# Turning the S5 states back on TensorE: four products in 64-row tiles instead of two after a VectorE combination, and the norm's squares summed on TensorE, in a two-block network on one Trainium2 core

## The chip, the cores and the metric

The kernel runs on one NeuronCore of a Trainium2 chip. The metric is device microseconds of one execution. The kernel before takes 1884.67 us (median of 3 runs, 1882.24 to 1885.48). The engines are called PE (TensorE matmuls), PEld (TensorE weight loads), DVE (VectorE), ACT (ScalarE), POOL (GpSimd) and SP (SyncE, here a DMA queue).

## The reference, cut to what matters

Two blocks of two layers each run one after the other on a state of 512 tokens by 1024 channels. The change touches the end of the first block (a residual and an RMS norm with the gain of `final_norm`) and the S5 mixer that follows it:

```
bur = einsum('gnh,btgh->btgn', bb_r, uc)          # 64 groups, 16 inputs, 64 complex states each
bui = einsum('gnh,btgh->btgn', bb_i, uc)
pr, pi, sr, si = associative_scan(combine, (ar, ai, bur, bui), axis=1)   # x[t] = a * x[t-1] + bu[t], complex
y = einsum('ghn,btgn->btgh', c_re, xr) - einsum('ghn,btgn->btgh', c_im, xi)
y = gelu(y + d * u);  ab = y @ w_glu;  mix = ab[..., :dm] * sigmoid(ab[..., dm:])
```

In front of the mixer stand two norms in a row, so that two sums over the 1024 channels are needed for each token: of the squares, and of the squares times the squared gain `g_fin1`.

## The kernel before, in words

Channels lie on partitions, tokens along the free axis, in tiles of 128 by 512. Large products are made by `mm3` (lines 308 to 310): three fp32r matmuls of 128x128 weights on 512 columns (weights and inputs each split into a high and a low part). Weights come through SP's queue into two `raw` buffers (line 288), ACT makes the high part (line 249), DVE or POOL the low part (line 252), each in 3 buffers.

The stages are `even` (conv and pool mixer), `odd` (LRU mixer), `s5`, `glu`, and then MLP, gate, attention, MLP, gate and the last norm. While `even` runs, `tables` builds the S5 tables in DRAM for 8 feature tiles `ft` of 8 groups each: `tS` (inputs to states), `tM` (inputs to outputs inside a chunk), `tR` (rotations: cosine and sine for each of 64 chunks) and `tO` (states to outputs). `tO` is written by `stored` (line 1072) on SP's queue, 8 DMAs of 64 KB per `ft`, so that the real states of two groups and their imaginary states stand on 128 rows.

The last part of `odd` makes 8 output tiles `m`, 36 matmuls each. `odd_out` adds the residual on DVE, turns the tile and writes it through DRAM to make `U[m]` (the S5 input), and squares it twice on ACT, once plain and once with the gain; DVE adds each square to one of two running sums `acc12`. In `s5`, behind four filler blocks of 6 matmuls (`fillers`: the projections for the gate stages), `columns` (line 368) sums the two over the partitions with 8 matmuls of one column; then a chain of small DVE operations makes the norm factors, eight matmuls spread them (line 1197) and the tiles `U` are scaled.

`s5` then goes through `ft` = 0..7. `states(ft)` has 16 matmuls on PE (line 1251: fp32, 128 rows by 64 weight columns, on 64 columns), which leave the real parts (r = 0) and the imaginary parts (r = 1) of the chunk inputs in PSUM, the even group of a pair on rows 0 to 63 and the odd one on rows 64 to 127. DVE rotates them with `C` and `N` (three multiplications, an addition, a subtraction), scans them (line 1266), and turns them back: three multiplications into `c` and `b`, a memset, and four additions or subtractions of 64 rows each that write into another half of the rows. These build `e`: for each half `q` of the groups the real states on rows 0 to 63 and the imaginary ones on rows 64 to 127. `leave(ft)` adds, for each of the 8 groups g = 2*a4 + q, the products M*u (line 1291) and O*e (line 1293) in PSUM, two matmuls each (64 output rows `f` a time), and ACT makes the gelu. The result goes through DRAM (`dy`) and is split for the `glu` products.

The order on PE is written down by hand with `self.after()` (an instruction stands behind the last one of PE issued so far): states(0), three blocks, states(1), leave(0), a block, states(2), leave(1), a block, and so on; behind leave(5) and later the first `glu` products (`part`) stand as well. Within these bounds a scheduler sets the order. DVE's `states(ft)` is kept behind all of `states(ft - 1)`.

Of the kernel before, what the change touches and what calls it, by code (L numbers as in the profile page):

```python
# [11 lines left out]
AF = mybir.ActivationFunctionType  # L12
# [156 lines left out]
class Kern:  # L169
# [238 lines left out]
    def consts(self):  # L408
        nc = self.nc
        self.vecs = self.p_const.tile([128, self.I["vecs"].shape[1]], F32, name="vecs")  # L410
        nc.sync.dma_start(out=self.vecs, in_=self.I["vecs"])
        ct = self.p_const.tile([128, self.I["consts"].shape[1]], F32, name="ctile")
        nc.scalar.dma_start(out=ct, in_=self.I["consts"])
        C = lambda n: ct[:, self.cat[n][0]:self.cat[n][0] + self.cat[n][1]]
        self.ident, self.fix, self.eye16, self.chunk, self.not0 = (C(n) for n in ("ident", "fix", "eye16", "chunk", "not0"))
        self.half, self.own = C("half"), C("own")
        self.halfpi = self.p_const.tile([128, 1], F32, name="halfpi")
        nc.gpsimd.memset(self.halfpi, 1.5707963267948966)
        self.ones = self.p_const.tile([128, 128], F32, name="ones")
        nc.vector.memset(self.ones, 1.0)  # L420

        o = self.bank("st")
        for _ in range(self.WARM):
            nc.tensor.matmul(o[:, 0:128], self.ones, self.ones, start=True, stop=True)

        warm = self.p_const.tile([128, 1], F32, name="warm")
        self.act(warm, self.halfpi, AF.Silu)
        self.tab, self.U, self.acc12 = [], [], []
        self.ft, self.behind, self.ticks = None, [], 0


# [301 lines left out]
    def odd(self, h):  # L733
# [42 lines left out]
        for ms in self.ODD_MS:  # L776
            os = {m: self.bank(("mm", "mm", "mm", "sp", "sp", "yp", "yp", "mm")[m]) for m in ms}
            for q in range(2):
                for m in ms:
                    w = self.get_w()  # L780
                    for k in range(6):
                        self.mm3(os[m], w, k, ysp[6 * q + k], q + k == 0, q == 1 and k == 5)
                    if q == 1:
                        out[m] = self.odd_out(m, os[m], h[m])
        return out

    def lru(self, x, i, gt):
# [25 lines left out]
    def odd_out(self, m, o, h):  # L813

        n = self.H("h3")
        v = lambda a: a.rearrange("p (c s) -> p s c", s=8)
        self.add(n.rearrange("p (s c) -> p s c", s=8), v(o), v(h))
        if len(self.tab):


            r = self.L("xc", 2 + self.LAG)
            self.act(r.rearrange("p (s c) -> p s c", s=8), n.rearrange("p (s c) -> p s c", s=8)[:, ::-1], AF.Copy)
            du = self.dram.tile([128, T], F32, name=f"du{m}")
            self.nc.gpsimd.dma_start(out=du.rearrange("(s h) (g c) -> h g s c", s=8, g=8).rearrange("h g s c -> (h g) s c"),
                                     in_=r.rearrange("p (s c) -> p s c", s=8))
            U = self.p_xg.tile([128, 8, 64], F32, tag="xg", name="U")
            self.nc.gpsimd.dma_start(out=U.rearrange("p g c -> p (g c)"), in_=du)
            self.U.append(U)

            for k, g in enumerate((1.0, self.V("g_fin1", m))):  # L830
                q = self.L(*(self.sq if m else ("acc", 2)))
                self.act(q, n, AF.Square, scale=g)
                if m == 0:
                    self.acc12.append(q)
                else:
                    self.add(self.acc12[k], self.acc12[k], q)
        return n


# [19 lines left out]
    def odd_vectors(self):  # L859

        P = lambda nm, dt=F32: self.L("sv_" + nm, 1, dt, (128, 12))
        lam = self.V("lam", 0, 12)
        na, u, s, z, p, q = P("na"), P("su"), P("ss"), P("sz"), P("sp"), P("sq")
        self.act(na, lam, AF.Abs)
        self.ts(na, na, -1.0, ALU.mult)
        self.exp_small(na, 12, P, out=u)

        self.ts(q, u, 2.0, ALU.add)
        self.nc.vector.reciprocal(out=q, in_=q)
        self.mul(s, u, q)  # L870
        self.mul(z, s, s)
        self.ts(p, z, 1.0 / 15, ALU.mult)
        for c in (1 / 13, 1 / 11, 1 / 9, 1 / 7, 1 / 5, 1 / 3):
            self.stt(p, p, c, z, ALU.add, ALU.mult)
        self.stt(p, p, 1.0, s, ALU.add, ALU.mult)
        self.ts(q, lam, -1.0, ALU.mult, 0.0, ALU.max)
        self.stt(q, p, 2.0, q, ALU.mult, ALU.add)
        C = lambda nm, w: self.p_const.tile([128, w], F32, name=nm)
        self.sp4 = C("sp4", 12)
        self.ts(self.sp4, q, 4.0, ALU.mult)  # L880

# [95 lines left out]
    def tables(self, small):  # L977
# [16 lines left out]
        for ft in range(8):  # L994
# [14 lines left out]
            for q in range(2):  # L1009
# [58 lines left out]

                def stored(q=q, orr=orr, oi=oi, tO=tO):
                    for k, w in enumerate((orr, oi)):  # L1070
                        for g2 in range(2):
                            nc.sync.dma_start(out=tO[64 * k:64 * k + 64, 512 * q:512 * q + 512].rearrange("n (a g m) -> n g a m", a=2, g=2)[:, g2],
                                              in_=w[64 * g2:64 * g2 + 64].rearrange("p a j h -> p a (j h)"))

                late(stored)
                if q == 1:
# [77 lines left out]
    def s5(self, h, fill, glu):  # L1154
# [46 lines left out]
                behind(*next(blocks))  # L1201

        fillers(self.FILL[0])
        st = self.bank("st")
        for k in range(2):
            behind(self.columns, self.acc12[k], st, 4 * k)
        fillers(self.FILL[1])
        s = self.p_s.tile([128, 24], F32, tag="st", name="st_s")
        v, t = s[:, 0:8], s[:, 8:12]
# [30 lines left out]
        def states(ft):  # L1240
# [17 lines left out]
            else:  # L1258
                self.tt(a, sp, c2, ALU.mult)
            self.mul(b[:, 0], sp[:, 1], N)  # L1260
            self.mul(b[:, 1], sp[:, 0], N)
            self.add(a[:, 0], a[:, 0], b[:, 0])
            self.sub(a[:, 1], a[:, 1], b[:, 1])
            for r in range(2):
                z = a[:, r].rearrange("p a c -> p (a c)")
                nc.vector.tensor_tensor_scan(out=z, data0=dec.rearrange("p a c -> p (a c)"), data1=z, initial=0.0, op0=ALU.mult, op1=ALU.add)


            e, c = f4(), f4()
            self.tt(c, a, c2, ALU.mult)  # L1270
            self.mul(b[:, 0], a[:, 1], N, nc.gpsimd if ft in self.B0P else None)
            self.mul(b[:, 1], a[:, 0], N, nc.gpsimd if ft in self.B1P else None)
            nc.vector.memset(e[:, :, :, 0:1], 0.0)
            for r, op in ((1, ALU.add), (0, ALU.subtract)):
                for q in range(2):
                    rows = slice(64 * q, 64 * q + 64)
                    self.tt(e[64 * r:64 * r + 64, q, :, 1:64], c[rows, r, :, 0:63], b[rows, r, :, 0:63], op)
            live[ft] = O, M, u, e

        def leave(ft):  # L1280
            O, M, u, e = live.pop(ft)
# [2 lines left out]
            for q in range(2):  # L1284
                self.yps.append(self.bank("yp"))
                yp = self.yps[-1][:, 0:256].rearrange("p (a c) -> p a c", a=4)
                for a4 in range(4):
                    g = 2 * a4 + q
                    os = [yp[64 * f:64 * f + 64, a4, :] for f in range(2)]
                    for f, o in enumerate(os):  # L1290
                        nc.tensor.matmul(o, M[:, 128 * g + 64 * f:128 * g + 64 * f + 64], u[:, g, :], start=True, stop=False)
                    for f, o in enumerate(os):
                        nc.tensor.matmul(o, O[g // 4][:, g % 4, 64 * f:64 * f + 64], e[:, q, a4, :], start=False, stop=True)
                self.act(y.rearrange("p (a q) c -> p a q c", q=2)[:, :, q, :], yp, AF.Gelu_apprx_tanh)
            dy = self.dram.tile([128, T], F32, name=f"dy{ft}")
            nc.scalar.dma_start(out=dy, in_=y.rearrange("p g c -> p (g c)"))
# [533 lines left out]
```

## Time and profile before

| | |
|---|---|
| median of 3 runs | 1884.67 us (1882.24 to 1885.48) |
| the profiled execution | 1886.16 us, its span 1884.3 us |
| PE busy | 1764.2 us (94%), 9298 matmul records |
| DVE busy | 1167.2 us (62%) |
| ACT, POOL busy | 762.0 us (40%), 456.6 us (24%) |
| mean granted TensorE clock | 0.963 of 2.4 GHz |
| shares of the chain that ended last | PE 68%, DVE 14%, issue 5%, POOL 4%, ACT 4%, DMA 3% |

A row of the timeline gives the start and the duration of an instruction, its engine and source line, the tiles that it writes and reads, its shape and how many records the row merges; in brackets stands how long the engine had been idle and what released it. An fp32 matmul leaves two records, an fp32r matmul one: the 16 matmuls of `states` are a row of x32. A matmul's shape is written as rows of weights * columns of weights, then the rows and columns that it reads. `PEclk` in the table of stretches is the granted clock: 1.00 is 2.4 GHz, 0.50 is 1.2 GHz.

### The profile page before, as it was taken

What the parts mean: (1) busy time and instruction counts of PE and PEld (TensorE: products, weight loads), DVE (VectorE), ACT (ScalarE), POOL (GpSimd) and SP (SyncE); (2) the same over time, 40 slices, a digit from 0 to 9 for tenths busy, and PEclk for the clock granted to TensorE, in tenths of its full rate; (3) what the DMA queues carried; (4) which work ended last, traced back from release to release, by engine and by line L of the source; (5) the groups of instructions that cost most, each with busy time, mean ns of one, the idle gap of its engine ahead of it and who ended that gap; (6) DMA issues with size and microseconds to landing.
All of it is one profiled execution on the core that took longest, in us unless ns stands there. A gap on an engine that the chain in (4) does not pass through costs nothing.

```text
span 1884.3 us, 24650 instructions
## 1 busy us (share of the span) xinstructions
PE 1764.2 (94%) x9298; PEld 1439.7 (76%) x9298; DVE 1167.2 (62%) x1885; ACT 762.0 (40%) x1330; POOL 456.6 (24%) x422
## 2 busy tenths in 40 slices
PE   7797999999887897899999999998999999999997
PEld 5685778877765776687888888887778888888886
DVE  9989777555888859655432344578686642244456
ACT  4334444443554462234432332335665432233234
POOL 5464667333666643100000000032000000000002
PEclk8898999999988898899999999999999999999998
DMA  4598443331222488523232222333111233322322
GB/s 167 136 225 213 128 129 123 119 104 65 76 75 76 136 244 291 169 92 112 93 100 91 100 100 91 101 106 110 41 55 45 101 101 91 100 101 91 100 94 91
DMA packets 128871, 215.93 MB, mean 115 GB/s; under 512 B 40048, under 2 KB 79728, under 8 KB 128752
## 3 DMA queue, kind: packets, MB, share of 16 engines
q1 hardware_dynamic: 108144, 189.27, 32.5%
q10 hardware_dynamic: 17968, 16.43, 2.6%
q0 software_dynamic: 2640, 8.65, 1.4%
q8 instruction: 73, 1.20, 0.3%
q14 instruction: 46, 0.38, 0.1%
HBM read 187.44 MB, written 26.21 MB: 113 GB/s over the span
## 4 chain that ended last, share of the span: by engine, by line
PE 68%; DVE 14%; issue 5%; POOL 4%; ACT 4%; DMA 3%; SPq 1%; ACTq 0%; DVEq 0%; POOLq 0%
PE mm L308 19%; PE mm L310 19%; PE mm L309 19%; POOL lo L252 2%; DVE lo L252 1%; DVE e L808 1%; ACT hi L249 1%; PE pv L1609 1%; SPq L1175 1%; PE sc L309 1%; PE sc L308 1%; PE sc L310 1%; DVE pl L264 1%; DVE srm L267 1%; DVE h L264 1%
## 5 line engine op out<-in xcount | busy, mean ns | idle before, releaser
L249 ACT ACTIVATE hi<-raw 128x1024 fp32r<-128x1024 f32 (+1 forms) x280 | 292.4, 1046 | 672.8 <-PE mm L309 552.4
L252 DVE TENSOR_TENSOR lo<-raw,hi 128x1024 fp32r<-128x1024 f32 (+1 forms) x211 | 262.1, 1243 | 422.1 <-ACT hi L249 417.3
L310 PE MATMUL mm<-xg,lo 128*128 128x512 f32 x924 | 361.0, 391 | 9.4 <-DVE lo L252 8.1
L308 PE MATMUL mm<-xg,hi 128*128 128x512 f32 x924 | 363.2, 394 | 5.1 <-ACT hi L249 1.8
L309 PE MATMUL mm<-xg,hi 128*128 128x512 f32 x924 | 360.2, 390 | 0.3 <-DVE xg L252 0.2
L1423 POOL DMA_DIRECT2D pj<-proj x16 | 8.8, 549 | 1025.8 <-DVE t L264 784.0
L308 PE MATMUL mm<-hid,hi 128*128 128x512 f32 (+1 forms) x648 | 250.7, 387 | 1.8 <-DVE t L252 1.8
L309 PE MATMUL mm<-hid,hi 128*128 128x512 f32 (+1 forms) x648 | 250.3, 387 | 0.0
L310 PE MATMUL mm<-hid,lo 128*128 128x512 f32 (+1 forms) x648 | 250.1, 386 | 0.0
L310 PEld LDWEIGHTS mm<-xg,lo 128*128 128x128 f32 x924 | 173.8, 188 | 48.0 <-DVE lo L252 9.0
L308 PEld LDWEIGHTS mm<-xg,hi 128*128 128x128 f32 x924 | 173.8, 188 | 44.9 <-ACT hi L249 2.3
L252 POOL TENSOR_TENSOR lo<-raw,hi 128x1024 fp32r<-128x1024 f32 (+1 forms) x69 | 170.6, 2473 | 146.8 <-ACT hi L249 140.6
L309 PEld LDWEIGHTS mm<-xg,hi 128*128 128x128 f32 x924 | 173.8, 188 | 36.4 <-DVE xg L252 1.4
L308 PEld LDWEIGHTS mm<-hid,hi 128*128 128x128 f32 x648 | 121.7, 188 | 26.6 <-DVE t L252 2.0
L310 PEld LDWEIGHTS mm<-hid,lo 128*128 128x128 f32 x648 | 121.7, 188 | 24.6
L309 PEld LDWEIGHTS mm<-hid,hi 128*128 128x128 f32 x648 | 121.7, 188 | 24.6
L308 PE MATMUL mm<-y,hi 128*128 128x512 f32 x192 | 78.6, 409 | 10.2 <-ACT y L249 8.9
L309 PE MATMUL mm<-y,hi 128*128 128x512 f32 x192 | 76.8, 400 | 0.0
L310 PE MATMUL mm<-y,lo 128*128 128x512 f32 x192 | 76.5, 399 | 0.0
L309 PE MATMUL mm<-big,hi 128*128 128x512 f32 x160 | 64.5, 403 | 3.9 <-DVE big L264 3.9
L308 PE MATMUL mm<-big,hi 128*128 128x512 f32 x160 | 65.3, 411 | 2.2 <-ACT hi L249 2.2
L310 PE MATMUL mm<-big,lo 128*128 128x512 f32 x160 | 64.2, 402 | 0.1
(468 smaller groups left out, 3086.1 us busy)
## 6 DMA issues: line engine op xcount, KB each, us to landing
raw<-in_w_up SPq DMA_DIRECT2D x64, 512.0 KB
raw<-in_w_down SPq DMA_DIRECT2D x64, 512.0 KB
raw<-in_w_in_even SPq DMA_DIRECT2D x40, 512.0 KB
raw<-in_w_in_odd SPq DMA_DIRECT2D x24, 512.0 KB
raw<-in_w_out_even SPq DMA_DIRECT2D x16, 512.0 KB
raw<-in_w_glu SPq DMA_DIRECT2D x16, 512.0 KB
raw<-in_w_gate SPq DMA_DIRECT2D x16, 512.0 KB
raw<-in_w_out_odd SPq DMA_DIRECT2D x16, 384.0 KB
```

Source lines behind the costliest of these rows:

```text
L249: self.nc.scalar.activation(out=out, in_=in_, func=func, scale=scale, bias=bias)
L252: (eng or self.nc.vector).tensor_tensor(out=out, in0=a, in1=b, op=op)
L264: self.nc.vector.scalar_tensor_tensor(out=out, in0=a, scalar=s, in1=b, op0=op0, op1=op1)
L267: (eng or self.nc.vector).tensor_scalar(out=out, in0=a, scalar1=s1, scalar2=s2, op0=op0, **({} if op1 is None else {"op1": op1}))
L308: mm(out, hi[:, sl], xh, start=start, stop=False)
L309: mm(out, hi[:, sl], xl, start=False, stop=False)
L310: mm(out, lo[:, sl], xh, start=False, stop=stop)
L808: nc.vector.tensor_tensor_scan(out=y, data0=u[:, k], data1=x[:, k], initial=0.0, op0=ALU.mult, op1=ALU.add)
L1175: nc.sync.dma_start(out=M0[:, 128 * g:128 * g + 128], in_=bass.AP(k0.tensor, k0.offset + 4096 * g, [[16, 8], [256, 16], [1, 128]]))
L1423: self.nc.gpsimd.dma_start(out=p, in_=pj[m])
L1609: mm(o, l, r[:, w], start=n == 0, stop=n == 6 * nk - 1)
```

## The change

`states` keeps the turned states on their rows. The two tiles `c` (states times cosine) and `e` (states times plus or minus sine) are no longer combined on DVE: the memset and the four 64-row operations go, and the sign is put in by a scalar_tensor_tensor where a multiplication stood. The same is done at the first rotation, so that an addition and a subtraction of 256 columns become one addition of 512. `leave` adds up on PE what DVE combined: for each group and each output half `f`, the real rows of `c` and `e` with one half of `O`, the imaginary rows with the other, four matmuls with 64 rows of weights on 63 columns where there was one with 128 rows on 64. `tO` is written in the order in which its rows now stand, half as many DMAs. `odd_out` squares a tile once; four matmuls of two columns (ones, and the squared gain) sum it over the partitions in PSUM, over all 8 tiles.

```diff
@@ odd: behind the products of tile m
                         out[m] = self.odd_out(m, os[m], h[m])
+
+                        if m and self.squares:
+                            self.squares.pop(0)()
@@ odd_out
-            for k, g in enumerate((1.0, self.V("g_fin1", m))):
-                q = self.L(*(self.sq if m else ("acc", 2)))
-                self.act(q, n, AF.Square, scale=g)
-                if m == 0:
-                    self.acc12.append(q)
-                else:
-                    self.add(self.acc12[k], self.acc12[k], q)
+            q = self.L(*self.sq)
+            self.act(q, n, AF.Square)
+            if m == 0:
+                self.st12 = self.bank("st")
+            st = self.st12[:, 0:8].rearrange("p (j b) -> p b j", j=2)
+
+            def summed():
+                for b in range(4):
+                    with self.after():
+                        self.nc.tensor.matmul(st[:, b], q[:, 128 * b:128 * b + 128], self.g12[:, m], start=m + b == 0, stop=m == 7 and b == 3)
+
+            self.squares.append(summed)
@@ odd_vectors
+        self.g12 = C("g12", 16).rearrange("p (k j) -> p k j", j=2)
+        nc = self.nc
+        nc.vector.memset(self.g12[:, :, 0:1], 1.0)
+        self.mul(self.g12[:, :, 1], self.V("g_fin1", 0, 8), self.V("g_fin1", 0, 8))
@@ tables: stored
                     for k, w in enumerate((orr, oi)):
-                        for g2 in range(2):
-                            nc.sync.dma_start(out=tO[64 * k:64 * k + 64, 512 * q:512 * q + 512].rearrange("n (a g m) -> n g a m", a=2, g=2)[:, g2],
-                                              in_=w[64 * g2:64 * g2 + 64].rearrange("p a j h -> p a (j h)"))
+                        nc.sync.dma_start(out=tO[:, 512 * k + 256 * q:512 * k + 256 * q + 256], in_=w.rearrange("p a j h -> p (a j h)"))
@@ s5
         fillers(self.FILL[0])
-        st = self.bank("st")
-        for k in range(2):
-            behind(self.columns, self.acc12[k], st, 4 * k)
+        for f in self.squares:
+            f()
+        st = self.st12
         fillers(self.FILL[1])
@@ s5: states
             self.mul(b[:, 0], sp[:, 1], N)
-            self.mul(b[:, 1], sp[:, 0], N)
-            self.add(a[:, 0], a[:, 0], b[:, 0])
-            self.sub(a[:, 1], a[:, 1], b[:, 1])
+            self.stt(b[:, 1], sp[:, 0], -1.0, N, ALU.mult, ALU.mult)
+            self.add(a, a, b)
...
-            e, c = f4(), f4()
+            c, e = f4(), f4()
             self.tt(c, a, c2, ALU.mult)
-            self.mul(b[:, 0], a[:, 1], N, nc.gpsimd if ft in self.B0P else None)
-            self.mul(b[:, 1], a[:, 0], N, nc.gpsimd if ft in self.B1P else None)
-            nc.vector.memset(e[:, :, :, 0:1], 0.0)
-            for r, op in ((1, ALU.add), (0, ALU.subtract)):
-                for q in range(2):
-                    rows = slice(64 * q, 64 * q + 64)
-                    self.tt(e[64 * r:64 * r + 64, q, :, 1:64], c[rows, r, :, 0:63], b[rows, r, :, 0:63], op)
-            live[ft] = O, M, u, e
+            self.stt(e[:, 0], a[:, 1], -1.0, N, ALU.mult, ALU.mult)
+            self.mul(e[:, 1], a[:, 0], N)
+            live[ft] = O, M, u, (c, e)
@@ s5: leave
                     for f, o in enumerate(os):
                         nc.tensor.matmul(o, M[:, 128 * g + 64 * f:128 * g + 64 * f + 64], u[:, g, :], start=True, stop=False)
-                    for f, o in enumerate(os):
-                        nc.tensor.matmul(o, O[g // 4][:, g % 4, 64 * f:64 * f + 64], e[:, q, a4, :], start=False, stop=True)
+
+                    rows = slice(64 * q, 64 * q + 64)
+                    for r in range(2):
+                        for x in e:
+                            for f, o in enumerate(os):
+                                nc.tensor.matmul(o[:, 1:64], O[r][rows, a4, 64 * f:64 * f + 64], x[rows, r, a4, 0:63], start=False, stop=r == 1 and x is e[1], tile_position=(64 * q, 64 * f))
```

Three places in the order of the instructions carry the prediction. The first is PE at `states(2)` and `leave(1)`: `mm<-y` is a filler block, `sp<-U` the states, `yp<-U` the products M*u, `yp<-xs` those of the turned states; the last number is the count of matmuls. Of before:

```order
L310 MATMUL mm<-y,lo 128x512
L1251 MATMUL sp<-U,x 64x64 x16
L1291 MATMUL yp<-U,gt 64x64 x4
L1293 MATMUL yp<-xs,O 64x64 x2
L1291 MATMUL yp<-U,gt 64x64 x2
```

and of the change:

```order
L310 MATMUL mm<-y,lo 128x512
L1261 MATMUL sp<-U,x 64x64 x16
L1294 MATMUL yp<-U,gt 64x64 x2
L1300 MATMUL yp<-xs,O 64x63 x8
L1294 MATMUL yp<-U,gt 64x64 x2
```

The alternation goes on so for all 8 groups: two matmuls M*u and two O*e by turns before, two M*u and eight O*x now. M*u has 128 rows of weights in both; O has 128 rows before and 64 now.

The second place is DVE in one `states` (`xs<-sp` and `xs<-xs,y` are the multiplications with the rotation, line 1266 and then 1275 is the scan). Of before:

```order
L252 TENSOR_TENSOR xs<-sp,y 128x512
L252 TENSOR_TENSOR xs<-sp,y 128x256 x2
L252 TENSOR_TENSOR xs<-xs 128x256 x2
L1266 SCALAR_TENSOR_TENSOR xs<-xc,xs 128x256 x2
L252 TENSOR_TENSOR xs<-xs,y 128x512
L1273 MEMSET xs 128x8
L252 TENSOR_TENSOR xs<-xs 64x4x63 x4
```

and of the change:

```order
L252 TENSOR_TENSOR xs<-sp,y 128x512
L252 TENSOR_TENSOR xs<-sp,y 128x256
L264 SCALAR_TENSOR_TENSOR xs<-sp,y 128x256
L252 TENSOR_TENSOR xs<-xs 128x512
L1275 SCALAR_TENSOR_TENSOR xs<-xc,xs 128x256 x2
L252 TENSOR_TENSOR xs<-xs,y 128x512
L264 SCALAR_TENSOR_TENSOR xs<-xs,y 128x256
L252 TENSOR_TENSOR xs<-xs,y 128x256
```

Before, two more multiplications of 256 columns stand around the last of 512. Memset and the four 64-row operations are gone.

The third place is PE in the last part of `odd` and behind it (`st` is the bank of the norm sums). Before, the sums stand once, behind the fourth filler block:

```order
L308 MATMUL mm<-y,hi 128x512
L309 MATMUL mm<-y,hi 128x512
L310 MATMUL mm<-y,lo 128x512
L368 MATMUL st<-ones,acc 128x1 x8
L308 MATMUL mm<-y,hi 128x512
```

and of the change such a group of four stands behind the products of each tile m from 1 to 7, and the last behind the fourth filler block:

```order
L308 MATMUL mm<-y,hi 128x512
L309 MATMUL mm<-y,hi 128x512
L310 MATMUL mm<-y,lo 128x512
L842 MATMUL st<-g_628,xr 128x2 x4
L308 MATMUL mm<-y,hi 128x512
```

32 matmuls instead of 8, 28 of them between the products of `odd`.

## Rows read from the trace of the kernel before

**Rows 1.** The page, busy time of the engines over the whole span.

```profile
PE 1764.2 (94%) x9298; PEld 1439.7 (76%) x9298; DVE 1167.2 (62%) x1885; ACT 762.0 (40%) x1330; POOL 456.6 (24%) x422
```

**Rows 2.** Stretches of the `s5` stage: from and to (us), length, then busy time (records) of PE, PEld, DVE, ACT and POOL, the granted clock, the share of the DMA engines, GB/s.

```profile
722.00:728.70 6.70, 0.70 (x24) 0.56 (x20) 6.62 (x10) 1.35 (x2) 2.42 (x2) 0.91 0.92 323
728.70:734.60 5.90, 5.87 (x62) 4.90 (x62) 5.80 (x15) 0.77 (x2) 0.00 (x0) 0.52 0.41 152
741.64:751.70 10.06, 4.75 (x102) 4.01 (x102) 9.96 (x16) 1.37 (x3) 4.51 (x4) 0.99 0.93 270
769.00:776.20 7.20, 0.43 (x3) 0.01 (x1) 5.30 (x10) 1.54 (x2) 1.10 (x2) 0.70 0.78 205
```

**Rows 3.** The timeline of DVE, one `states` from its first rotation to `e`.

```profile
735.80 1.35 DVE L252 TENSOR_TENSOR xs<-sp,y 128x512 f32<-128x512 f32 x3 [0.42 <-PE sp L1251]
737.08 0.75 DVE L252 TENSOR_TENSOR xs<-xs 128x256 f32<-128x256 f32 x2
737.74 1.27 DVE L1266 TENSOR_TENSOR_SCAN xs<-xc,xs 128x256 f32<-128x256 f32 x2
738.93 1.33 DVE L252 TENSOR_TENSOR xs<-xs,y 128x256 f32<-128x256 f32 x3
740.22 0.07 DVE L1273 MEMSET xs<- 128x8 f32 x1
740.30 1.74 DVE L252 TENSOR_TENSOR xs<-xs 64x252 f32<-64x252 f32 x4
```

**Rows 4.** The timeline of PE at the same place: a filler block, `states`, `leave`, and the next block.

```profile
737.55 0.50 PE L308 MATMUL mm<-y,hi 128*128 128x512 f32 x1
...
739.14 1.15 PE L1251 MATMUL sp<-U,x 128*64 128x64 f32 x32
740.13 0.40 PE L1291 MATMUL yp<-U,e 128*64 128x64 f32 x8
741.64 0.34 PE L1293 MATMUL yp<-xs,i 128*64 128x64 f32 x4 [1.11 <-DVE xs L252]
741.81 0.29 PE L1291 MATMUL yp<-U,e 128*64 128x64 f32 x4
741.92 0.29 PE L1293 MATMUL yp<-xs,i 128*64 128x64 f32 x4
...
743.21 0.29 PE L1293 MATMUL yp<-xs,i 128*64 128x64 f32 x4
743.42 0.50 PE L308 MATMUL mm<-y,hi 128*128 128x512 f32 x1
```

**Rows 5.** The waits of PE from 690 to 900 us: line, whom it waited for, us in total, times, the longest.

```profile
PE yp L1293 <- DVE xs L252: 13.5, 4, 6.0
```

**Rows 6.** The timeline of PE in the attention stage, where the tiles' rows change between 128 and 64, and in front of it, where only the type of the data changes (line 1609 is fp32r, line 1586 fp32, line 1551 bf16).

```profile
1370.20 0.28 PE L1609 MATMUL pv<-pt,vl 128*128 128x256 f32 x1
1370.32 1.04 PE L1586 MATMUL tp<-ctile,P 128*128 128x128 f32 x8
1371.19 0.38 PE L1551 MATMUL sc<-mask,idb 128*128 128x512 bf16 x1
1371.50 0.38 PE L1555 MATMUL sc<-k,q 64*128 64x256 f32 x1
1371.73 0.28 PE L1556 MATMUL sc<-k,q 64*128 64x256 f32 x1
```

**Rows 7.** The timeline of PE: the convolution's matmuls in tiles of 32 weight columns, and two rows of `leave(0)`, which lies in the second stretch of rows 2.

```profile
101.58 2.75 PE L534 MATMUL cv<-big,gt 128*32 128x128 f32 x96
...
729.00 0.43 PE L1291 MATMUL yp<-U,gt 128*64 128x64 f32 x4
729.21 0.43 PE L1293 MATMUL yp<-xs,i 128*64 128x64 f32 x4
```

**Rows 8.** The last part of `odd` as a stretch (columns as in rows 2), one-column sums at full clock in the MLP stage (timeline of PE), and the end of `odd` (a row of the timeline and a piece of the chain that ended last: start, us, what).

```profile
660.00:690.00 30.00, 30.00 (x133) 24.55 (x133) 16.52 (x19) 16.87 (x27) 16.93 (x15) 1.00 0.79 230
...
884.64 0.39 PE L310 MATMUL mm<-xg,lo 128*128 128x512 f32 x1
884.86 0.95 PE L368 MATMUL st<-ones,acc 128*128 128x1 f32 x8
...
886.00 0.40 PE L309 MATMUL mm<-xg,hi 128*128 128x512 f32 x1
...
702.81 0.50 PE L308 MATMUL mm<-y,hi 128*128 128x512 f32 x1 [1.77 <-ACT y L249]
...
705.09 3.21 PE st L368 x16
```

**Rows 9.** The timeline of PE at the first and behind the last `leave`, and of DVE at the split of the last S5 tile.

```profile
728.73 0.48 PE L1293 MATMUL yp<-xs,i 128*64 128x64 f32 x4 [6.03 <-DVE xs L252]
...
789.37 0.50 PE L308 MATMUL mm<-y,hi 128*128 128x512 f32 x1
...
795.61 0.69 DVE L252 TENSOR_TENSOR y<-acc,y 128x512 fp32r<-128x512 f32 x1 [5.32 <-ACT y L249]
```

**Rows 10.** The instructions of the line that stores `tO` (count: duration in ns, least/median/most, first and last start), a piece of the chain that ended last, and a stretch of `even` (columns as in rows 2).

```profile
L1072 SPq DMA_DIRECT2D tO<-tq_wr x32: 577/587/1778, 82.1 to 366.5; - x32
...
150.53 3.40 DMA tO<-tq_wr
...
150.00:200.00 50.00, 37.14 (x405) 30.47 (x405) 40.15 (x101) 22.61 (x66) 19.05 (x21) 0.86 0.78 202
```

More of the change, by code (lines that the diff above doesn't have):

```diff
@@ L427, in consts @@
         self.act(warm, self.halfpi, AF.Silu)
-        self.tab, self.U, self.acc12 = [], [], []
+        self.tab, self.U, self.squares = [], [], []
         self.ft, self.behind, self.ticks = None, [], 0
```

## The prediction

> **What bounds the kernel now.** I read the busy times first: PE works for 94% of the span [rows 1], so a change pays only where PE stands idle or where it takes work from PE. Then I read the stretches of the S5 stage, where the change sits: PE is idle for most of 722.0 to 728.7 (0.70 us busy of 6.70), half idle from 741.64 to 751.70, idle from 769.0 to 776.2 (0.43 of 7.20), while DVE is busy 6.62 of 6.70 and 9.96 of 10.06 us in the first two [rows 2]. The waits say the same: PE waited 13.5 us in four long waits for the turned states of DVE [rows 5]. So today the S5 loop runs at DVE's pace, and the stage lasts, on PE, from the first product with turned states at 728.73 to the block behind the last leave at 789.37 [rows 9]. Behind it PE is saturated and the last S5 tile, split at 795.61 [rows 9], finds it busy with other `glu` products; what the stage gains or loses I carry to the end.
>
> **What the change takes from DVE.** One `states` costs DVE 1.35 + 0.75 + 1.27 + 1.33 + 0.07 + 1.74 = 6.5 us [rows 3]. Memset and 64-row operations go: 1.8 us for each `ft`, 14.5 us in all. The sign costs nothing (a multiplication of the same size becomes a scalar_tensor_tensor), and one addition of 512 for two of 256 is taken at the same 0.75. There remain 4.7 us for each `ft`, plus the weight splits in between.
>
> **What it puts on PE in `leave`.** Before, 32 matmuls (64 records); now 16 of M*u and 64 of O*x, 160 records. Four records follow one another 0.11 to 0.12 us apart at full clock (741.81 to 741.92 for four), 32 records of `states` take 0.99 us with their start (739.14 to 740.13) [rows 4]; I take 28.8 ns a record. Narrower tiles with more columns go no faster: 96 records in 2.75 us are 28.6 ns each [rows 7]. So 63 columns instead of 64, or four tiles at once, buy nothing: 160 x 28.8 ns = 4.61 us.
>
> The second part is what I rest the forecast on. The size of the tile now changes between 128 rows (M*u) and 64 rows (O*x) with every group, 15 times in a leave. The attention stage shows what that costs elsewhere [rows 6]. Between line 1609 and 1586, and 1586 and 1551, only the data type changes and nothing is lost (eight records from 1370.32 to 1371.19). But line 1551 (512 columns, 0.21 us at full clock, so over at 1371.40) is followed by its first 64-row tile only at 1371.50, and the next one comes 0.23 us later although the same pair is later 0.11 apart: the weights were not loaded ahead. The way from 64 weight columns to 128 shows the same gap: the last four records at 743.21 end at 743.325, and line 308 starts at 743.42 [rows 4]. A gap of 0.095 us, then; the first load of 64 columns that isn't hidden adds 0.055 (741.64 to 741.81 is 0.17, against 0.115) [rows 4]. I take 0.15 us a change: 15 x 0.15 = 2.25 us. Between 0 (no row shows this very pair, 128 and 64 rows with 64 weight columns in both) and 0.20 are the bounds. The Trainium skill ("TensorEngine Tiling (Array Packing)", Key Properties) says that a change of the tiling mode drains the engine and a change of tile alone does not; by that rule the groups pay, and the trace agrees for the pairs that it has.
>
> A leave is then 4.61 + 2.25 = 6.86 us, three and a half times what it was (741.64 to 743.3 behind its first M*u, [rows 4]). Its 14.5 us less on DVE are paid with about 40 us more on PE, which has some 21 us idle in the stage.
>
> **The new S5 stage, walked through on PE.** The first turned states are ready 1.8 us earlier, at 726.9 instead of 728.73 [rows 9]. PE has waited 5 us by then, and behind the wait of before the granted clock was 0.52 [rows 2], with four records 0.21 us apart instead of 0.115 [rows 7]; I take 2.5 us more for the first leave (bounds 0, if the clock stays, and 4.5, if all of it runs so). It ends at 726.9 + 6.86 + 2.5 = 736.3. Then PE has no more reason to wait, since a round of it is longer than DVE's 4.7 us and a split: five blocks at 1.59 (737.55 to 739.14 [rows 4]) are 7.95; a double block 3.2; six matmuls of `glu` 1.6; the spread of the norm factor 0.9 (as the eight records of [rows 8]); six `states` at 0.99 are 5.9; seven leaves 48.0; seven gaps behind a leave 0.7. Together 68.3, so the block behind the last leave stands at 804.6 instead of 789.37: **15.2 us later**.
>
> **The squares.** Four matmuls of few columns push the products behind them back by 0.90 us: from line 310 at 884.64 to line 309 at 886.00 are 1.36 us, less two matmuls of 0.23 [rows 8]. Seven such groups, 6.3 us, fall into the last part of `odd`, where PE is busy 30.00 of 30.00 us [rows 8]. Against it: one ACT square and two DVE additions fewer for each tile; PE's wait of 1.77 us at 702.81 for an ACT that was late [rows 8] goes, as PE arrives later; the 16 records at 0.20 us each, 3.21 us on the chain that ended last [rows 8], become 8 for 0.9 us. 6.3 - 1.8 - 2.3 leaves 2.2 us, and I let the shorter way through ACT and DVE to the last tile's sum take these back: 0 for the start of S5. Bounds: 3 us earlier (all of the 6.3 hidden) and 6 us later (nothing of it). Each group waits for a square that ACT has made a tile earlier; what stands behind it on PE is the next tile's products, 4 us of work, so no wait is added.
>
> **The stores of `tO`.** 64 issues of 0.59 us on SP's queue become 32, 19 us less on that queue between 82 and 369 us; a store is on the chain that ended last (3.40 us at 150.53), because the tables' buffers wait for it. In that region PE is idle 12.9 of 50 us [rows 10]. I take 2 us of gain; bounds 0 and 12.9.
>
> **The sum**, against the profiled execution of 1886.16 us: + 15.2 + 0 - 2.0 = 1899.4. That execution was 1.5 us above the median of the runs (1884.67), so I forecast **1898**; with the bounds of its terms (change of tile 0.10 to 0.20, first leave 0 to 4.5, start -3 to +6, stores) this case reaches from 1889 to 1907.
>
> **Rivals.**
> *A, no price for the change of tile rows* (faster). The 120 changes cost nothing, because both kinds have 64 weight columns and no row shows this pair apart. Then 120 x 0.15 = 18 us less: 1880. PE still sets the pace (7.2 us a round), but all the idle time is used. For it: the waits for DVE [rows 5] vanish for certain, and DVE is the bound today. Against it: the gap is there where the rows of the tile alone change [rows 6]. The case turns at 0.045 us a change. Chance 20%.
> *B, records at 53 ns* (much slower). Four records in 0.21 us at a clock of 0.52 are this cadence [rows 2, 7]; if the leaves with their gaps keep PE at that level, or if two weight loads of 64-row tiles don't overlap, seven leaves cost 160 x 25 ns = 4 us more each: 1926. Against it: the dense small matmuls ran at 28.8 [rows 4]. The Trainium skill ("TensorE: Matmul & The Clock Gate", LDWEIGHTS) gives a load as its columns over 1.2 GHz, an estimate of 53 ns for 64; the row of 28.8 ns says that here loads overlap. Chance 8%.
> *C, the front gives back more*: the stores were what PE waited for in `even`, and all 12.9 us [rows 10] come back instead of 2: 1887. For it speaks the store on the chain; against it that most of that stretch's chain is DVE and POOL work. Chance 8%.
>
> **The numbers.** The forecast has the remaining 64%. A difference under 0.2%, about 3.8 us, is what a measurement of this kernel cannot tell from no change. Of A 14 points are faster and 6 within, of C 5 within and 3 slower; 2 points are added to faster for a forecast with every term at its lower end and C in part. Faster 16%, same 11%, slower 73%. The range takes in A with 3 us below it and the forecast to 1907 with 7 us for a first leave and a start both at their ends: 1877 to 1914; B is left out.
>
> **What would show it right or wrong.** In the stretch from 727 us PE is busy without a long wait and DVE falls to some 60% busy; the waits for turned states shrink to the first one. A leave lasts 6.5 to 7.5 us at full clock, with a gap of about 0.1 us whenever line 1294 and 1300 follow each other; if these gaps are under 0.02 us, A holds, and if eight records of line 1300 take 0.43 us, B. The last leave ends near 804 (plus what the front moved). The squares' line 842 takes 0.9 us for four matmuls. If `leave(0)` begins more than 4 us before or after 727, my zero for the squares is wrong.

## The result and the profile after

The changed kernel takes 1908.26 us (median of 4 runs, 1905.92 to 1910.31) against 1883.45 us before (4 runs beside it, 1881.87 to 1885.48): a ratio of 1.0127, interval 1.0113 to 1.0141, so slower by about 24 us. The forecast was 1898 us. The direction and the mechanism hold. The sum fell short: it had 13.3 us over the kernel before, so about 10.6 us of the loss were missing. The profiled execution took 1907.53 us.

The page's busy times of after, to be read against [rows 1]:

```profile
PE 1802.6 (95%) x10114; PEld 1470.4 (77%) x10114; DVE 1142.2 (60%) x1825; ACT 757.6 (40%) x1322; POOL 458.5 (24%) x422
```

DVE works 25 us less, PE 38 us more, in 816 more records. The waits of PE between 700 and 830 us (line, whom it waited for, us in total, times, the longest) and stretches of S5 (columns as in [rows 2]):

```profile
PE st L1207 <- DVE xc L252: 3.7, 1, 3.7
PE yp L1300 <- DVE xs L252: 2.6, 1, 2.6
```

```profile
727.00:730.50 3.50, 0.87 (x30) 0.73 (x26) 3.50 (x4) 1.47 (x2) 1.78 (x2) 1.00 0.74 283
730.50:739.60 9.10, 9.08 (x152) 7.61 (x152) 5.23 (x11) 0.38 (x1) 0.00 (x0) 0.60 0.33 119
750.00:770.00 20.00, 20.00 (x414) 16.67 (x412) 10.50 (x19) 3.96 (x8) 2.37 (x3) 1.00 0.67 195
```

The 13.5 us of waits for turned states [rows 5] have shrunk to one of 2.6 us; from 730.5 to 830 us PE waits for nobody, and DVE is busy 10.50 of 20 us where it was busy 9.96 of 10.06 [rows 2]. The bound has moved from DVE to PE. What PE does there shows in its timeline: the start and end of one leave at full clock (start, us, engine, line, operation, count).

```profile
752.99 0.29 PE L1294 MATMUL yp<-U,e 128*64 128x64 f32 x4
753.21 0.68 PE L1300 MATMUL yp<-xs,i 64*64 64x63 f32 x16
753.82 0.34 PE L1294 MATMUL yp<-U,e 128*64 128x64 f32 x4
...
754.69 0.34 PE L1294 MATMUL yp<-U,e 128*64 128x64 f32 x4
...
759.34 0.68 PE L1300 MATMUL yp<-xs,i 64*64 64x63 f32 x16
759.95 0.50 PE L308 MATMUL mm<-y,hi 128*128 128x512 f32 x1
```

From one M*u to the next are 0.87 us (753.82 to 754.69) for 20 records. At 28.8 ns they are 0.576 us; the other 0.295 us are two changes of tile rows, 0.147 us each. The leave lasts 6.96 us up to the block behind it: 160 records and 16 such changes, the last of them to the block. Before, the products behind the first M*u took 1.7 us [rows 4]. DVE's side, one `states`:

```profile
754.12 1.02 DVE L252 TENSOR_TENSOR xs<-sp,y 128x512 f32<-128x512 f32 x2
...
758.48 0.42 DVE L252 TENSOR_TENSOR xs<-xs,y 128x256 f32<-128x256 f32 x1
762.73 0.69 DVE L252 TENSOR_TENSOR xs<-sp,y 128x512 f32<-128x512 f32 x1 [3.84 <-PE sp L1261]
```

It is 4.8 us from 754.12 to 758.9 instead of 6.5 [rows 3], and then DVE stands 3.84 us idle until PE has the next states: the roles are exchanged. The rows of PE that answer to [rows 9]:

```profile
730.52 1.00 PE L1300 MATMUL yp<-xs,i 64*64 64x63 f32 x28 [2.65 <-DVE xs L252]
...
810.61 0.50 PE L308 MATMUL mm<-y,hi 128*128 128x512 f32 x1
...
812.12 0.39 PE L308 MATMUL mm<-y,hi 128*128 128x512 f32 x1
```

The first product with turned states comes 1.79 us later than before, the block behind the last leave 21.24 us later (810.61 against 789.37). By that block PE has run fewer of the `glu` products than before: the product that starts at 789.37 us before starts at 812.12 here, 22.7 us later. At their ends the two profiled executions differ by 21.4 us.

### The profile page after: what moved, and what is told of

The parts are those of the page before. It is cut to its first block, busy times and chain, and to the rows that moved or that the text cites. A ratio compares the mean times of both kernels' runs of the same rounds, so it can differ in the third digit from the quotient of the medians.

```text
span 1905.7 us, 26168 instructions
## 1 busy us (share of the span) xinstructions
PE 1802.6 (95%) x10114; PEld 1470.4 (77%) x10114; DVE 1142.2 (60%) x1825; ACT 757.6 (40%) x1322; POOL 458.5 (24%) x422
## 3 DMA queue, kind: packets, MB, share of 16 engines
q1 hardware_dynamic: 103536, 189.27, 32.7%
## 4 chain that ended last, share of the span: by engine, by line
PE 70%; DVE 16%; issue 4%; POOL 4%; ACT 3%; DMA 2%; SPq 0%; ACTq 0%; DVEq 0%; POOLq 0%
PE mm L308 19%; PE mm L310 19%; PE mm L309 19%; PE yp L1300 2%; POOL lo L252 2%; DVE lo L252 1%; DVE e L811 1%; PE pv L1616 1%; ACT hi L249 1%; PE yp L1294 1%; DVE srr L252 1%; PE sc L309 1%; PE sc L310 1%; PE sc L308 1%; DVE srm L267 1%
```

## The experiments

Eleven kernels, in three groups, each timed beside the kernel before on the same chip. The difference in us is the ratio less one, times 1884 us; its interval reaches some 2 to 4 us to either side. M*u and O*x are the products of line 1294 and line 1300 of after.

| kernel | ratio to before | interval | about us |
|---|---|---|---|
| after | 1.0127 | 1.0113 to 1.0141 | +24 |
| e1, squares alone | 1.0016 | 1.0002 to 1.0030 | +3.0 |
| e2, turned states alone | 1.0110 | 1.0092 to 1.0127 | +20.7 |
| e3, all M*u first | 1.0074 | 1.0054 to 1.0093 | +14 |
| e4, DVE adds | 1.0081 | 1.0061 to 1.0101 | +15 |
| e5, e3 + e4 + old squares | 0.9988 | 0.9978 to 0.9999 | -2.3 |
| e6, e5 half by half | 1.0005 | 0.9990 to 1.0021 | +0.9 |
| e7, 128 rows for O*x | 1.0045 | 1.0026 to 1.0064 | +8.5 |
| e8, stores cut in two | 1.0131 | 1.0112 to 1.0150 | +25 |
| e9, e1 in one pass | 1.0009 | 1.0000 to 1.0018 | +1.7 |
| e10, e5 + e9's sums | 1.0007 | 0.9997 to 1.0016 | +1.3 |
| e11, e5 + split on GpSimd | 0.9986 | 0.9976 to 0.9996 | -2.6 |

**e1: the squares alone.** The kernel before, with this part of the change and nothing else (shown in part):

```diff
-            for k, g in enumerate((1.0, self.V("g_fin1", m))):
...
+            q = self.L(*self.sq)
+            self.act(q, n, AF.Square)
...
+                        self.nc.tensor.matmul(st[:, b], q[:, 128 * b:128 * b + 128], self.g12[:, m], start=m + b == 0, stop=m == 7 and b == 3)
```

> Before, with only the new sums of the squares (TensorE's 32 small products a block instead of ScalarE's second square and the DVE adds); the leave and the states stay as they were. The prediction's term for this part was zero: the time of before, 1883.5 us. The rival, read from the trace of after: the norm's chain in front of S5 starts later and the first states come some 3 to 5 us later, so 1887 to 1889 us.

Measured +3.0 us, interval 0.4 to 5.7, so that zero is just outside it: the prediction's zero for this part was wrong. The rival has the size; whether it has the reason is taken up at e9.

**e2: the turned states alone.** The reverse edit in after (shown in part):

```diff
-        for f in self.squares:
-            f()
-        st = self.st12
+        st = self.bank("st")
+        for k in range(2):
+            behind(self.columns, self.acc12[k], st, 4 * k)
```

> After, with the old sums of the squares: only the turned states and the 64-row products are left of the change. If the squares cost 3 to 5 us, as the trace of after reads, 1903 to 1905 us; if they cost nothing, 1908 us as after. If e1 and this one together make less or more than after's 24.8 us over before, the two parts share a wait.

Measured a ratio of 1.0110. The two parts add up: 1.0016 and 1.0110 make 1.0126, after has 1.0127. So no wait that both share shows, to within some 4 us, and some seven eighths of the loss are the turned states: 20.7 us, interval 17 to 24. The prediction had 15.2 us for them, and 13.2 with its gain from the stores, which e2 also has.

**e7: no change of tile rows.** One line of after; the same 160 records in the same order, and the products of O take both groups' rows (so it computes other sums than the reference):

```diff
-                                nc.tensor.matmul(o[:, 1:64], O[r][rows, a4, 64 * f:64 * f + 64], x[rows, r, a4, 0:63], start=False, stop=r == 1 and x is e[1], tile_position=(64 * q, 64 * f))
+                                nc.tensor.matmul(o[:, 1:64], O[r][:, a4, 64 * f:64 * f + 64], x[:, r, a4, 0:63], start=False, stop=r == 1 and x is e[1], tile_position=(0, 64 * f))
```

> After, with the products of O taken over all 128 rows in place of 64 (same number of records, same order, same 64 columns; each product takes in the other group's rows too, so the sums differ from the reference's). Theory (the change of tile rows costs 0.15 us): the gaps go and a leave falls from 7.0 to 4.7 us, so 1889 to 1892 us. Rival (the gap belongs to the alternation between M and O, or to the number of records): no change, 1908 us. A third: 128 rows cost more per record (53 instead of 28.8 ns), then a leave is 8.5 us and the time 1920 us.

The timeline of PE in e7:

```profile
744.61 0.29 PE L1294 MATMUL yp<-U,e 128*64 128x64 f32 x4
744.73 0.64 PE L1300 MATMUL yp<-xs,i 128*64 128x63 f32 x16
745.20 0.29 PE L1294 MATMUL yp<-U,e 128*64 128x64 f32 x4
...
748.81 0.64 PE L1300 MATMUL yp<-xs,i 128*64 128x63 f32 x16
749.38 0.50 PE L308 MATMUL mm<-y,hi 128*128 128x512 f32 x1
```

A group of 20 records now takes 0.58 to 0.59 us instead of 0.87, that is 29 ns a record and no gap; the leave 4.77 us. Only the rows that a tile takes differ, so the gap belongs to them, and neither to the alternation nor to the count. That 128 rows would make a record dearer is excluded. Eight leaves save 15 x 0.147 x 8 = 17.6 us; the time falls by 15.4, which agrees within the interval. What is left fits the waits: PE now waits 5.9 us for turned states instead of 2.6 (the row below), since its round has come near DVE's.

```profile
PE yp L1300 <- DVE xs L252: 5.9, 2, 3.2
```

**e3: all M*u first.** The same products, reordered:

```diff
-                    os = [yp[64 * f:64 * f + 64, a4, :] for f in range(2)]
-                    for f, o in enumerate(os):
-                        nc.tensor.matmul(o, M[:, 128 * g + 64 * f:128 * g + 64 * f + 64], u[:, g, :], start=True, stop=False)
-
-                    rows = slice(64 * q, 64 * q + 64)
+                    for f in range(2):
+                        with self.after():
+                            nc.tensor.matmul(yps[q][64 * f:64 * f + 64, a4, :], M[:, 128 * g + 64 * f:128 * g + 64 * f + 64], u[:, g, :], start=a4 == 0, stop=False)
+            for q in range(2):
+                rows = slice(64 * q, 64 * q + 64)
+                for a4 in range(4):
                     for r in range(2):
```

> After, with the same products in another order: all 16 records of M*u of a tile first, then all 64 products of O, so that the rows of the tile change once or twice in a leave instead of 15 times. Theory (a change of tile rows costs 0.15 us, a record 28.8 ns): a leave falls from 7.0 to about 5.0 us, eight leaves save some 14 to 17 us: 1891 to 1894 us. Rival (only the number of records counts, and the gaps are something else, such as the start of a bank): no change, 1908 us.

PE in e3, and the wait that is new there:

```profile
746.95 1.10 PE L1295 MATMUL yp<-U,e 128*64 128x64 f32 x32
747.99 3.77 PE L1303 MATMUL yp<-xs,i 64*64 64x63 f32 x128
751.69 0.50 PE L308 MATMUL mm<-y,hi 128*128 128x512 f32 x1
```

```profile
PE yp L1295 <- ACT xr L249: 3.1, 1, 3.1
```

The leave is 4.74 us. Its 128 records of O*x take 3.70 us up to the block, the change in front of the block included, so at most 28.9 ns each, though halfway the tiles move from rows 0 to 63 to rows 64 to 127: moving a tile of the same size costs nothing, changing its size costs 0.147 us. The Trainium skill ("TensorEngine Tiling (Array Packing)", Key Properties) makes just this difference, a change of mode draining the engine and a change of tile not; the trace agrees on both: a gap of 0.147 us at the one, none at the other.

The time falls by 10 us (5 to 15 with the intervals), where 14 to 17 were expected; no change, the rival, is excluded. Two things in the trace can take the difference: a leave that needs both banks at its start waits 3.1 us for ScalarE's Gelu, and the granted clock. The stretch from 727 to 800 us of four kernels (columns as in [rows 2]; the third number from the end is the clock), after first, then e3, e4, e7:

```profile
727.00:800.00 73.00, 70.35 (x1378) 58.38 (x1376) 43.46 (x69) 14.22 (x26) 15.13 (x14) 0.93 0.60 189
```

```profile
727.00:800.00 73.00, 67.78 (x1541) 60.81 (x1536) 45.07 (x72) 14.53 (x26) 14.47 (x13) 0.88 0.66 200
```

```profile
727.00:800.00 73.00, 69.11 (x952) 53.61 (x949) 50.24 (x81) 15.12 (x27) 14.31 (x13) 0.84 0.64 195
```

```profile
727.00:800.00 73.00, 66.98 (x1556) 60.01 (x1552) 45.25 (x73) 15.28 (x29) 14.99 (x13) 0.95 0.67 205
```

At a mean clock of 0.93 the equivalent of 0.07 x 73 = 5.1 us of full clock is lost in this stretch, at 0.88 it is 8.8, at 0.84 11.7, at 0.95 3.7. For e3: eight leaves of 4.74 instead of 6.96 us are 17.8 us less; without 3.7 for the clock and 3.1 for the bank 11.0 are left; measured 10. Such sums go by one execution of each kernel.

**e4: DVE adds again.** Half the records of O*x, the 15 changes kept:

```diff
-            live[ft] = O, M, u, (c, e)
+            self.add(c, c, e)
+            live[ft] = O, M, u, (c,)
```

> After, but DVE adds the two turned tiles (one more add of 512 columns, about 0.7 us a tile), so TensorE takes half of the 64-row products: 64 records fewer in a leave, the 15 changes of tile rows stay. Theory (28.8 ns a record plus 0.15 us a change): a leave falls from 7.0 to about 5.1 us and stays longer than DVE's share, eight leaves save about 14 us: 1893 to 1896 us. Rival (DVE's turned states are the bound again once they take 5.2 us): less than half of that, 1901 us or more.

PE in e4, one leave and stretches:

```profile
749.75 0.29 PE L1295 MATMUL yp<-U,e 128*64 128x64 f32 x4
...
750.34 0.34 PE L1295 MATMUL yp<-U,e 128*64 128x64 f32 x4
750.61 0.45 PE L1301 MATMUL yp<-xs,i 64*64 64x63 f32 x8
750.98 0.34 PE L1295 MATMUL yp<-U,e 128*64 128x64 f32 x4
...
754.84 0.50 PE L308 MATMUL mm<-y,hi 128*128 128x512 f32 x1
```

```profile
766.00:769.00 3.00, 3.00 (x60) 2.35 (x58) 2.90 (x6) 0.39 (x1) 0.00 (x0) 1.00 0.96 324
769.00:775.00 6.00, 6.00 (x36) 4.70 (x34) 1.27 (x3) 1.93 (x3) 1.74 (x2) 0.50 0.85 246
789.00:796.00 7.00, 7.00 (x41) 5.04 (x40) 6.25 (x8) 0.68 (x2) 2.29 (x2) 0.53 0.50 181
```

The leave is 5.09 us, as the theory said: a group of 12 records takes 0.64 us (750.34 to 750.98), 12 x 28.8 ns and again 0.295 us. But the time falls by 8.7 us (4 to 13) where 14 was expected. The rival's reason is not it: behind the first product PE waits for DVE nowhere. What the trace shows instead is the clock. Its mean of 0.84 costs 6.6 us more than after's 0.93; 64 records fewer in each of eight leaves are 14.7 us, and 14.7 - 6.6 = 8.1. Both new stretches at the lower level (0.50 and 0.53) come while PE is busy the whole time. No run here changes the clock alone, so this is read from a trace and not tested.

**e5, e6 and e11: a version that beats both?** e5 puts e3's order, e4's add and e2's old squares together; e6 is e5 with each half's O*x right behind its own M*u; e11 is e5 with one more tile split on GpSimd (`if ft < 7` for `if ft < 6`).

> Three edits at once against after: all M*u of a tile first (as e3), DVE's add (as e4), and the old sums of the squares (as e2). Theory: a leave is 96 records and two changes, about 3.1 us; DVE's states are 5.2 us instead of 6.5 us as before, and DVE is the bound again: up to 10 us under before, 1874 to 1880 us. Rival (what e3's trace shows: a leave that needs both banks at its start waits for ScalarE, which waits in its own queue for a transfer, some 3 us and a stretch at the lower clock): 1881 to 1887 us, no gain over before.

> As e5, but half by half: the 8 products M*u of a bank, its 16 products of O, then the other bank's, so that a leave starts with one free bank and has three changes of tile rows (0.3 us a leave more than e5). Theory (the wait for the bank is what e3 and e5 lose): 1873 to 1879 us, and no worse than e5. Rival (the wait only moves behind the first half, or DVE is the bound anyway): the time of e5 within 2 us.

> e5, with the split of the seventh y tile on GpSimd, as for the six before it, instead of ScalarE and DVE. In e5 ScalarE waits 6.0 us at 779.8 us for that tile's transfer, with the Gelu of the last tile behind it in its queue. Theory (the wait holds up work that TensorE needs): 1 to 4 us under e5. Rival (nothing waits for ScalarE there that is not hidden behind the blocks of the last part): as e5.

The timeline of PE in e5, its waits inside S5, and a stretch of S5:

```profile
747.38 1.10 PE L1284 MATMUL yp<-U,u 128*64 128x64 f32 x32
750.37 1.91 PE L1292 MATMUL yp<-xs,O 64*64 64x63 f32 x64 [1.88 <-DVE xs L252]
752.21 0.50 PE L308 MATMUL mm<-y,hi 128*128 128x512 f32 x1
```

```profile
PE yp L1292 <- DVE xs L252: 7.0, 4, 3.5
PE mm L308 <- ACT y L249: 4.9, 1, 4.9
```

```profile
740.00:770.00 30.00, 26.04 (x552) 22.10 (x550) 29.28 (x47) 8.48 (x16) 6.85 (x7) 0.94 0.91 271
```

A leave of e5 costs PE 1.03 us of M*u and 1.84 us of O*x, and DVE is the bound again (29.28 of 30.00 us). Against e2 the eight leaves cost PE 32.7 us less ((6.96 - 2.87) x 8), and the time falls by 23. The rest, 9.7 us, fits what PE now waits inside S5: 7.0 and 4.9 us here, 2.2 in e2. The time is 2.3 us under before, the interval just under 1, where the expectation had up to 10. The rival of e5 gave the right size, not the reason: no wait for a bank is left in e5, but four waits for DVE (7.0 us) and one of 4.9 us for a block's input, behind which ScalarE had waited 4.7 us for a transfer. e6 is some 3 us slower than e5, though their intervals touch: its theory is excluded, and its rival's 2 us are not quite met. e11 is the same as e5, as its rival had it. With PE at 26 and DVE at 29 of 30 us, and the DMA engines at 0.91, these shares leave little to shift in this stage.

**e8: the stores.** Each store of `tO` cut in two, the layout kept:

```diff
-  nc.sync.dma_start(out=tO[:, 512 * k + 256 * q:512 * k + 256 * q + 256], in_=w.rearrange("p a j h -> p (a j h)"))
+  for g2 in range(2):
+      p = slice(64 * g2, 64 * g2 + 64)
+      nc.sync.dma_start(out=tO[p, 512 * k + 256 * q:512 * k + 256 * q + 256], in_=w[p].rearrange("p a j h -> p (a j h)"))
```

> After, with each store of tO cut in two (64 rows each), so that there are 8 stores a tile again as before, with the same layout. If fewer, larger stores gave something back in the front (the prediction took 2 us for it, bound 12.9), this is 2 us or more slower than after: 1910 us. If the front's gain is zero, as the trace of after reads, 1908 us.

The same ratio as after (1.0131 and 1.0127) within some 4 us: the 12.9 us of rival C are excluded, a gain of 2 us is not. The traces show none either. At the product that before starts at 647.05 us, ahead of the squares, the nine kernels with the fewer stores lie between 2.8 us ahead of before and 1.4 behind it (mean 0.6 ahead), and e1 and e9, with the old stores, 1.6 ahead and 0.9 behind.

**e9 and e10: the price of the squares.** e9 is e1 with `q` and the two columns in the one-pass type, which halves the records (shown in part; the two sums also stand in another order in their bank):

```diff
-            q = self.L(*self.sq)
+            q = self.L(*self.sq, F32R)
```

> As e1 (before, with only TensorE's sums of the squares), but the squares and the two columns they are multiplied by are of the one-pass type (fp32r) instead of fp32, so that each of the 32 products is one record instead of two. Theory (the squares cost because their products stand in a stretch where TensorE is never idle; e1 falls some 8 us behind there and a later wait gives part of it back): the lag halves to some 4 us and the time is that of before within 1.5 us, 1884 to 1886 us. Rival (what costs is the later start of the norm's chain, since the last sum waits for the last square): as e1, about 3 us over before.

> e5's leave (M*u first, DVE's add) with e9's sums of the squares. If e9's sums cost nothing, the time of e5, some 2 us under before; if ScalarE's and DVE's work that the sums take away is worth something in front of S5, up to 2 us less than e5, 1880 us; if they cost what they cost in e1, 1885 us.

The timeline of PE at the same sum (tile 6) in e1 and in e9:

```profile
701.38 0.95 PE L842 MATMUL st<-g,xr 128*128 128x2 f32 x8
702.19 0.49 PE L308 MATMUL mm<-y,hi 128*128 128x512 f32 x1
```

```profile
706.16 0.50 PE L842 MATMUL st<-g12r,xr 128*128 128x2 f32 x4
706.52 0.49 PE L308 MATMUL mm<-y,hi 128*128 128x512 f32 x1
```

Every kernel here issues the 2240 products of line 308 in the same sequence of blocks, so the same product can be found in two traces and its lag read. From the product that before starts at 662.30 us to the one at 688.38, e1 falls 7.9 us behind, after 7.0, e9 3.7; with the old squares (e2, e5) it is 1.4 and 0.3. Six groups of sums lie in it, at 0.81 us each in e1 (701.38 to 702.19), 4.9 us. Most of the rest is waiting, which before does not have in this stretch. The waits of PE in e1 from 655 to 705 us:

```profile
PE mm L310 <- POOL lo L252: 1.1, 1, 1.1
PE st L842 <- ACT xr L249: 0.7, 2, 0.4
```

In e9 a group costs 0.36 us (706.16 to 706.52), and the lag is half. The total falls too, from +3.0 to +1.7 us, but the intervals overlap (0.4 to 5.7 and 0 to 3.4). This speaks for the sums' time on PE rather than for the norm's later start, without settling it. e10 does not fit as well: with one-pass sums the time of e5 grows by 0.0019, 3.6 us, with interval ends that allow 1 to 6. How much of this belongs to the sums alone is open; that they gain nothing is shown.

## Why the prediction came out as it did

**The bound moves to PE: right.** The long waits for DVE are gone, DVE idles, and PE is full from 730.5 us on. e7, e3 and e4 take from PE each a known amount, and the time follows it as far as clock and new waits let it.

**The leave, 6.86 us: right.** It is 6.96 with the gap behind it, for which the walk had another 0.1. The cadence of 28.8 ns and the 0.15 us a change were both read from rows of before [rows 4, 6, 7], the second from pairs that were not the same; in after it is 0.147, and e7 shows that it is due to the rows of the tile alone. Rival A (no price) is refuted by this, and rival B (53 ns a record) by the cadence at full clock.

**The first leave, 2.5 us for the clock: right in size, but ended too early.** From the first turned product to the block behind this leave are 9.1 us, where the walk had 9.36. But the lower level went on behind it. The block and the `states` that follow, in after:

```profile
739.63 0.79 PE L308 MATMUL mm<-y,hi 128*128 128x512 f32 x1
...
742.49 1.15 PE L1261 MATMUL sp<-U,x 128*64 128x64 f32 x32
```

The block took 2.86 us where the walk has 1.59: 1.3 us that it did not have.

**The walk through S5, 15.2 us: too short by 5.5, the largest miss.** The walk adds up to the block behind the last leave and compares it with 789.37 us. Between its first turned product and that moment the kernel before had run 58 matmuls of blocks and `glu`; the walk has 48 (five blocks and the `glu` group of 6 each, a double block of 12), and after ran 53. The ten that the walk leaves out must be run all the same, 2.3 us at 0.23 each. e2 measures this part of the change by itself, 20.7 us where the sum has 15.2. In its trace, PE:

```profile
728.39 1.00 PE L1288 MATMUL yp<-xs,i 64*64 64x63 f32 x28 [2.21 <-DVE xs L252]
...
737.06 0.79 PE L308 MATMUL mm<-y,hi 128*128 128x512 f32 x1
...
739.92 1.67 PE L1249 MATMUL sp<-U,x 128*64 128x64 f32 x32
...
808.56 0.50 PE L308 MATMUL mm<-y,hi 128*128 128x512 f32 x1
```

Of the 5.5 us between the two the ten products are 2.3, and the first turned product 1.5, since it stands at 728.39 and not at 726.9. The clock has about 1: the first leave is 0.7 shorter than in the walk (8.67 us), the block and the `states` behind it 1.8 longer. The rest is open.

**The squares, zero: wrong.** The prediction had 6.3 us on PE, and took off 1.8 and 2.3 for a wait and for the old sums; the 2.2 us that remained it "let the shorter way through ACT and DVE" take back. e1 gives +3.0: the remainder was real, and no row shows what would take it back. The seven groups cost 0.81 us each, 5.7 us, a little less than the 6.3; but that "no wait is added" was wrong too, since two of the first groups waited 0.7 us for their squares. The prediction's own sign, a `leave(0)` that begins more than 4 us from 727, was too coarse: its first turned product came 3.5 us after 727, and it was e1 that showed the term. In the trace of after the last sum is the thing that the norm waits for, and then PE waits for the norm (DVE, then PE):

```profile
711.07 0.16 DVE L267 TENSOR_SCALAR st_s<-st 128x4 f32<-128x4 f32 x1 [4.91 <-PE st L842]
```

```profile
717.61 0.46 PE L1207 MATMUL st<-ctile,xc 128*32 128x64 f32 x16 [3.69 <-DVE xc L252]
```

DVE had stood idle 4.91 us, so what ScalarE and DVE save here lies where neither is the limit.

**The stores, 2 us of gain: not seen.** e8 and the traces show none, though 2 us is too little for the ratio to exclude. The queue's issues did fall. DVE's waits for the tables' buffers behind these stores rose (5.8 and 1.5 us before, 20.4 after), but that does not set the time either: in e8 they are 8.1 us at the same time. A store on the chain that ended last was no evidence that fewer stores shorten the chain. Rival C is refuted.

**The sum.** By the medians the forecast was 13.3 us over before, and 24 were measured (21 to 27). Of the 10.6 us between them the turned states have 5.5 (e2), the squares 3.0 (e1), and the gain of the stores that did not come 2. In single executions the places ahead of the squares already scatter by some 2 us (at the product of 647.05 us of before, after stands 1.4 us later, and e1, which has the old leave, 1.6 earlier), so the 1.5 us of the first turned product above may be no more than that. The time, 1908, lies just outside the bounds of the forecast's own case (1889 to 1907); the wider range, to 1914, holds it.

## What to carry to other kernels

Before work is handed from the engine that waits least to the one with idle gaps, compare the sum, not the gaps: here 1.8 us a tile less on DVE cost 5 us a tile more on PE, which could hide only about half of it in its idle time. Count for small products of 64 columns the records, whether their tile has 64 or 128 rows, and the changes of tile size between them; where they must be mixed, put all products of one size together, since that alone was worth 10 of 24 us here. A term with a remainder that "something will take back" is a cost until a row shows what takes it. And when a walk is compared with a time of the old trace, the same products must lie in front of both: here ten were missing, 2.3 us.

## What the runs showed that was not expected

- The granted clock fell to its lower level (0.50 from 769 to 775 us in e4) behind three microseconds in which PE had been busy all the time at full clock. The idle time before a leave is not the only thing that brings it down, and in that execution 6.6 of the 14.7 us that lighter PE work saved went back that way.
- A record with 63 columns costs some 29 ns whether its weights have 64 or 128 rows (at most 28.9 ns in e3, 29 in e7): taking half the rows saved nothing.
